# Prompt attention on one core: value products of a unit in one run, a unit later, with wider exponentials and score tiles in a borrowed ring

## The chip, the cores and the metric

One core of a Trainium2 chip runs the whole kernel in one launch. The metric is the device time of the kernel in microseconds (us). The times shown are the median of three timed runs, beside one execution that the hardware profiler recorded. PE is TensorE (matmuls), PEld its weight loads, DVE is VectorE, ACT ScalarE, POOL GpSimd and SP SyncE, which issues most DMAs.

## What is computed

One inference step of a decoder layer. 2048 prompt tokens and 8 x 8 new tokens go through one input projection, then through two groups of heads in parallel (eight forgetting-attention heads of width 64, four mLSTM heads of width 128), an output projection, LayerNorm and an MLP. The change concerns the prompt's attention:

```python
s = jnp.einsum('bqhd,bkhd->bhqk', q_i, k).astype(jnp.float32) * scale
s = s + L_i[..., :, None] - L[:, :, None, :]          # L: running sum of the log forget gate
s = jnp.where(k_pos[None, :] <= q_pos[:, None], s, -jnp.inf)
p = jax.nn.softmax(s, axis=-1)
return jnp.einsum('bhqk,bkhd->bqhd', p.astype(v.dtype), v)
```

The new tokens attend to 8192 cached positions each, whose pages are gathered from memory. That stream of gathers runs beside the other stages.

## The kernel before

The stages follow one another: input projection with the mLSTM scan beside it (phase A), prompt attention (phase B), output projection (phase O), MLP (phase C). The program is written with a tile scheduler: the order of the instructions on each engine is decided when the kernel is built, from the order in the source, the room in the pools and a model of time; on the chip each engine works through its own list and waits where a semaphore says so.

**Phase B** (`phase_b`) works in 64 units, one for a head h and a group g of 256 queries (two tiles of 128). In loop round n it computes `scores` of unit n and `values` of unit n - 1 (`LA = 1`).

- `scores(z, g)`: for each of the two query tiles, keys in blocks of 512. Two matmuls a block (L1074, L1075; the query is split into a high and a low part) go into a PSUM bank `pS`, of which three are in turn. DVE adds the forget term and takes the row's maximum on the way into an SBUF tile `S` (L1081; L1085 for the diagonal block). `S` tiles have 512 columns and ten buffers. POOL prepares the diagonal's mask `nd` (L1067).
- `values(z, g, sc)`: ACT takes the exponential of each `S` tile in place, up to 512 columns at a time, with the row's sum (L1100). Then, for each four key tiles: PE transposes four 128 x 128 weights into a PSUM bank `pt` (L1113, three banks), ACT or DVE copies them to an SBUF tile `PT` (L1116, L1118; four buffers), and PE multiplies them with the values `vn` (L1122). Key tile k adds to the lower 64 partitions of `po` if k is even, to the upper 64 if it is odd (`c = (k % 2) * 64`). A unit has nk = 2g + 2 key tiles, so 2 to 16 value products, 576 in all; the last one covers only the second query tile (128 columns). At the end the halves are added (L1128, L1130), and after four units `finish` divides by the sums and stores.
- Beside them stand the loads and splits of the next unit's queries (`queries`) and the transposes and splits of the next head's keys (`keys`, L1030).

Two things of other stages are issued from the loop. `kx["ring"]` (six slots of 1024 columns) belongs to the stream of cached keys; the first six gathers into it (L1637, on POOL) go out one in each of the rounds 10 to 15, and the stream goes on in phase O. Four loads of `w_o` (L1213, on SP) into the pool `raw()` (`wr`, four buffers of 1024 columns) are asked for in round 12; phase O starts with them, as with the loads of `xr` from `dmix` (L1268).

Of the kernel before, what the change touches and what calls it, by code (L numbers as in the profile page):

```python
# [10 lines left out]
F32 = mybir.dt.float32  # L11
# [14 lines left out]
S = 2048  # L26
# [26 lines left out]
def body(ctx, tc, I, O, stages):  # L53
    nc = tc.nc
    V, A, G, T, SY = nc.vector, nc.scalar, nc.gpsimd, nc.tensor, nc.sync
# [20 lines left out]
    ident = cst.tile([128, 128], F32, name="ident")  # L76
# [24 lines left out]
    acc = [0.0, None, PACE_A, None]  # L101
    macc = [0.0, [], PACE_M]
    last = {}

    vx = dict(more=None, live=[], next=0, of={})
    kx = dict(ring=None, new=False, free=False)
# [7 lines left out]
    def beside(gen):  # L114

        with ExitStack() as es:
            for i in last.values():
                es.enter_context(tc.issue_after(i.ins))
            return next(gen, 0)

    def attend():

        r = beside(acc[1])
        if r == 3:
            acc[3] = acc[1]
        if r in (0, 3):
            acc[1] = None

    def tick(us):

        macc[0] += us
        while macc[1] and macc[0] > macc[2]:
            macc[0] -= macc[2]
            if beside(macc[1][0]) == 0:
                macc[1].pop(0)
        if not macc[1]:
            macc[0] = 0.0
        acc[0] += us
        while acc[1] is not None and acc[0] > acc[2]:
            acc[0] -= acc[2]  # L140
            attend()
# [817 lines left out]
    for bi in range(4):  # L959
        g = block_a(bi)  # L960
# [18 lines left out]
    def phase_b():  # L979
        es = ExitStack()  # L980
        pb = es.enter_context(tc.tile_pool(name="pb", bufs=1, reuse_waits="tile"))
        ppb = es.enter_context(tc.tile_pool(name="ppb", bufs=1, space=PSUM, reuse_waits="tile"))
# [69 lines left out]

        lastnd = [None]

        def scores(z, g):

            qh, ql = z.pop(("q", g))
            ks = z["ks"]
            forget = lambda a, b: Bz["nl"][:, a:b] if z["h"] == 0 and a < 512 else z["nl"][:, a:b]
            out = []  # L1060
            for i in range(2):
                qt = 2 * g + i
                n = (qt + 1) * 128
                qs = slice(i * 128, i * 128 + 128)
                mx = pb.tile([128, 8], F32, name="mx", bufs=8)
                nd = pb.tile([128, 128], F32, name="nd", bufs=3)
                lastnd[0] = G.tensor_tensor(nd, forget(qt * 128, n), dmask, op=OP.add)  # L1067
                st = []
                j = 0
                for a in range(0, n, 512):  # L1070
                    b = min(n, a + 512)
                    w = max(b - a, 256)
                    pS = bank()
                    T.matmul(pS[:, :w], qh[:, qs], ks[:, a:a + w], start=True, stop=False)  # L1074
                    last["PE"] = T.matmul(pS[:, :w], ql[:, qs], ks[:, a:a + w], start=False, stop=True)  # L1075
                    tick(0.42)
                    sp = pb.tile([128, 512], F32, name="S", bufs=10)
                    st.append(sp)
                    e = min(b, qt * 128)
                    if e > a:  # L1080
                        last["DVE"] = V.tensor_tensor_reduce(out=sp[:, :e - a], in0=pS[:, :e - a], in1=forget(a, e), scale=1.0, scalar=NEG,  # L1081
                                               op0=OP.add, op1=OP.max, accum_out=mx[:, j:j + 1])
                        j += 1
                    if b == n:
                        V.tensor_tensor_reduce(out=sp[:, e - a:b - a], in0=pS[:, e - a:b - a], in1=nd, scale=1.0, scalar=NEG,  # L1085
                                               op0=OP.add, op1=OP.max, accum_out=mx[:, j:j + 1])
                        j += 1
                V.tensor_reduce(mx[:, 7:8], mx[:, :j], axis=AX.X, op=OP.max, negate=True)  # L1088
                out.append((st, mx))
            return out  # L1090

        def values(z, g, sc):

            for i, (st, mx) in enumerate(sc):
                qt = 2 * g + i
                n = (qt + 1) * 128
                lp = pb.tile([128, 4], F32, name="lp", bufs=8)
                for k, sp in enumerate(st):
                    w = min(512, n - k * 512)
                    last["ACT"] = A.activation(sp[:, :w], sp[:, :w], AF.Exp, bias=mx[:, 7:8], accum_out=lp[:, k:k + 1])  # L1100
                V.tensor_reduce(z["ls"][:, qt:qt + 1], lp[:, :len(st)], axis=AX.X, op=OP.add)

            po = ppb.tile([128, 256], F32, name="po", bufs=1)
            nk = 2 * g + 2
            for k0 in range(0, nk, 4):
                PT = pb.tile([128, 4, 256], F32, name="PT", bufs=4)
                for i in range(2):
                    kk = min(4, 2 * g + i + 1 - k0)
                    if kk <= 0:
                        continue  # L1110
                    pt = ppb.tile([128, 4, 128], F32, name="pt", bufs=3)
                    for k in range(kk):
                        T.transpose(pt[:, k], sc[i][0][k0 // 4][:, k * 128:(k + 1) * 128], ident)  # L1113
                    dst = PT[:, :kk, i * 128:i * 128 + 128]
                    if i == 0 or (k0 // 4) % 2 != 0:
                        A.copy(dst, pt[:, :kk])  # L1116
                    else:
                        V.tensor_copy(dst, pt[:, :kk])  # L1118
                for k in range(k0, min(k0 + 4, nk)):
                    q0 = 128 if k == nk - 1 else 0  # L1120
                    c = (k % 2) * 64
                    last["PE"] = T.matmul(po[c:c + 64, q0:], z["vn"][:, k], PT[:, k - k0, q0:],  # L1122
                                          start=(k < 2), stop=(k >= nk - 2), skip_group_check=True)
                tick(0.45 * min(4, nk - k0))
            if g % 4 == 0:
                z["ot"] = pb.tile([64, 1024], F32, name="ot", bufs=2)
            od = z["ot"][:, (g % 4) * 256:(g % 4) * 256 + 256]
            A.copy(od, po[0:64])  # L1128
            q0 = 128 if g == 0 else 0
            V.tensor_tensor(od[:, q0:], od[:, q0:], po[64:128, q0:], op=OP.add)  # L1130
            if g % 4 == 3:
                finish(z, g // 4)
# [19 lines left out]
        units = [(h, g) for h in range(8) for g in range(8)]  # L1152

        Z = {0: dict(h=0)}
# [4 lines left out]
        V.memset(dmask, 0.0)  # L1159
        G.affine_select(dmask, dmask, pattern=[[-1, 128]], compare_op=OP.is_ge, fill=NEG, base=0, channel_multiplier=1)  # L1160
        keys(Z[0], 0, kn)
        sc = {}
        LA = 1
        for n in range(len(units) + LA):
            if 10 <= n < 16 and acc[1] is not None:

                with tc.issue_after(lastnd[0].ins):
                    attend()
            if n == 12:
                wo.extend(half_wo(0, q) for q in range(4))  # L1170
            if n < len(units):
                h, g = units[n]
                sc[n] = scores(Z[h], g)
                if h == 0 and g % 2 == 0 and g < 6:
                    keys(Z[0], g // 2 + 1)
                if h < 7:
                    if g == 3:
                        Z[h + 1] = head(h + 1)
                        forget_values(Z[h + 1], 0, S)
                    if g >= 4:  # L1180
                        keys(Z[h + 1], g - 4)
                if n + 1 < len(units):
                    queries(Z[units[n + 1][0]], units[n + 1][1])
            if n >= LA:
                h, g = units[n - LA]
                values(Z[h], g, sc.pop(n - LA))
        es.close()
        es_z.close()

# [12 lines left out]
    def raw():  # L1202

        return pcw.tile([128, 1024], F32, name="wr", bufs=4)
# [295 lines left out]
def sample_attention(tc, I, O, ps_, pps, cst, ident, sqk, dnl, dR, dmix, dqb, vx, kx, pe, ring_a):  # L1500
# [226 lines left out]
    def weights(b, u, hg):  # L1727

        z = state[b]
        if hg == 0:  # L1730
            z["PT"] = ps_.tile([128, 2, 4, 4, 4, 8], F32, name="PTs", tag="PTs", bufs=1)
        PT = z["PT"]
        p = pps.tile([128, 4, 128], F32, name="sT", tag="sX", bufs=1)
        for f in range(4):
            T.transpose(p[:, f], z["U"][u][:, hg, f].rearrange("p k t -> p (k t)"), ident)
        for f in range(4):
            (A.copy if f % 2 else V.tensor_copy)(PT[:, hg, f].rearrange("p g h q -> p h g q"),
                                                 p[:, f].rearrange("p (h g q) -> p h g q", g=4, q=8))
# [22 lines left out]
    def pv_step(b, kt, after):  # L1761
# [9 lines left out]
        for n, f in enumerate((1, 0)):  # L1771
            with ExitStack() as es:
                if after is not None:
                    es.enter_context(tc.issue_after(after.ins))
                for g in range(2):
                    for hg in range(2):
                        r = (g * 2 + hg) * 32
                        after_ = T.matmul(po[r:r + 32], z["PT"][:, hg, 2 * f + g, pg].rearrange("p h q -> p (h q)"),  # L1778
                                          vts[f][:, g, hg * 256:(hg + 1) * 256], start=(kt == 0 and n == 0),
# [117 lines left out]
```

## Time and profile before

| what | us |
| --- | --- |
| median of three timed runs | 3359.53 (3354.93 to 3370.77) |
| the profiled execution, its own time | 3340.76 |
| its span, first to last instruction | 3339.1 |
| prompt attention in it, by the first and last of its matmuls | 922 to 1365 |

How to read it: a line of a group shows line, engine, operation, what it writes and reads, shape and count, then its busy time in us and the mean of one in ns, then the engine's idle time ahead of it and what ended that. Value products and other full-precision products leave two records for one product. Matmul ends are modelled, so distances between starts say more than durations. A row of the timeline merges instructions of one line that follow each other; it shows the first start, the time from there to the last end, and the count of records.

### The profile page before, as it was taken

To read this page: it belongs to the slowest core of one execution; us is meant where nothing else is said; L and a number is where in the kernel's file an instruction comes from. 1 tells how busy PE (TensorE), PEld (TensorE's weight loads), DVE (VectorE), ACT (ScalarE), POOL (GpSimd) and SP (SyncE) were. 2 spreads that over 40 slices of the span, in tenths; PEclk is the share of its full clock that TensorE was granted. 3 is DMA by queue.
4 is the path that set the end of the run, shared out by engine and by line. 5 is a ranking of instruction groups with operands and counts; after the bars stand their busy time and mean duration, and the time that the engine had idled before them with its cause. 6 is when DMAs were issued, how large, how long until landed. Compare 5 with 4: busy or idle time off the path is not lost. (4 is left out here: it accounts for less than half of the span.)

```text
span 3339.1 us, 57487 instructions
## 1 busy us (share of the span) xinstructions
PE 3231.6 (97%) x21420; PEld 2604.3 (78%) x21420; DVE 2156.3 (65%) x5225; ACT 1413.0 (42%) x2990; POOL 869.9 (26%) x932
## 2 busy tenths in 40 slices
PE   9999999999989999999999998999999999999998
PEld 8998797887866666677777776777777777889997
DVE  6857667566477878655666667666676545755555
ACT  4444245344278888422333333232433333433332
POOL 0112122422332322376432324323243210100001
PEclk9999999999999999999999999999999999999999
DMA  5666765967652322587776768767678654442221
GB/s 174 166 189 187 219 207 186 300 218 233 213 167 81 91 76 58 200 293 255 278 265 240 247 216 301 271 238 254 233 244 312 200 172 142 154 140 82 89 83 67
DMA packets 427296, 646.24 MB, mean 194 GB/s; under 512 B 83148, under 2 KB 320016, under 8 KB 426120
## 3 DMA queue, kind: packets, MB, share of 16 engines
q1 hardware_dynamic: 350184, 363.09, 36.0%
q0 software_dynamic: 74304, 270.57, 22.0%
q10 hardware_dynamic: 2528, 8.91, 0.7%
q8 instruction: 169, 2.77, 0.3%
q14 instruction: 111, 0.91, 0.1%
HBM read 589.63 MB, written 52.83 MB: 192 GB/s over the span
## 5 line engine op out<-in xcount | busy, mean ns | idle before, releaser
L1458 DVE TENSOR_TENSOR y<-y,py 128x512 f32<-128x512 f32 x475 | 320.0, 680 | 275.6 <-PE py L159 260.5
L149 ACT ACTIVATE wh<-wr 128x1024 fp32r<-128x1024 f32 x268 | 279.5, 1057 | 511.5 <-PE py L159 262.2
L1643 DVE STREAM_TRANSPOSE kT<-kT 128x512 f32<-128x512 f32 x512 | 330.6, 685 | 206.2 <-DMA kT<-cache_k,idxK 205.3
L157 PE MATMUL ph<-x1h,wh 128*128 128x512 f32 (+1 forms) x1280 | 454.2, 355 | 3.0 <-ACT wh L149 2.3
L1637 POOL DMA_INDIRECT kT<-cache_k,idxK x256 | 270.7, 1057 | 715.5 <-PE sQ L1666 651.7
L159 PE MATMUL ph<-x1h,wl 128*128 128x512 f32 (+1 forms) x1280 | 451.6, 354 | 4.9 <-DVE wl L152 4.8
L158 PE MATMUL ph<-x1l,wh 128*128 128x512 f32 (+1 forms) x1280 | 453.8, 355 | 0.0
L157 PE MATMUL py<-wh,h 128*128 128x512 f32 x1024 | 406.5, 399 | 5.9 <-DVE y L1456 4.5
L158 PE MATMUL py<-wl,h 128*128 128x512 f32 x1024 | 400.9, 392 | 0.0
L159 PE MATMUL py<-wh,h 128*128 128x512 f32 x1024 | 400.9, 392 | 0.0
L152 DVE TENSOR_TENSOR wl<-wr,wh 128x1024 fp32r<-128x1024 f32 x268 | 336.0, 1259 | 88.4 <-PE ph L159 34.4
L157 PE MATMUL pm<-whi,xhT 128*128 128x256 f32 (+2 forms) x1040 | 303.1, 291 | 1.6 <-DVE xlT L152 1.0
L159 PE MATMUL pm<-whi,xlT 128*128 128x256 f32 (+2 forms) x1040 | 298.3, 287 | 0.0
L158 PE MATMUL pm<-wlo,xhT 128*128 128x256 f32 (+2 forms) x1040 | 298.1, 287 | 0.0
L157 PEld LDWEIGHTS ph<-x1h,wh 128*128 128x128 f32 x1280 | 241.6, 189 | 40.6 <-issue 4.1
L159 PEld LDWEIGHTS ph<-x1h,wl 128*128 128x128 f32 x1280 | 241.2, 188 | 40.1 <-DVE wl L152 6.6
L158 PEld LDWEIGHTS ph<-x1l,wh 128*128 128x128 f32 x1280 | 241.4, 189 | 35.5 <-issue 4.1
L157 PEld LDWEIGHTS py<-wh,h 128*128 128x128 f32 x1024 | 192.3, 188 | 61.1 <-issue 11.5
L159 PEld LDWEIGHTS py<-wh,h 128*128 128x128 f32 x1024 | 192.2, 188 | 45.1 <-issue 4.1
L158 PEld LDWEIGHTS py<-wl,h 128*128 128x128 f32 x1024 | 192.4, 188 | 35.8 <-DVE wl L152 0.4
L1100 ACT ACTIVATE S<-S,mx 128x512 f32<-128x512 f32 (+2 forms) x320 | 207.9, 653 | 18.5 <-DVE mx L1088 17.9
L1754 POOL DMA_INDIRECT vt<-cache_v,idxV x158 | 163.1, 1032 | 194.5 <-PE sO L1778 138.2
(410 smaller groups left out, 6668.5 us busy)
## 6 DMA issues: line engine op xcount, KB each, us to landing
wr<-w SPq DMA_DIRECT2D x256, 512.0 KB
wra<-w_in SPq DMA_DIRECT2D x112, 512.0 KB
Rb<-dR SPq DMA_DIRECT2D x128, 128.0 KB
wr<-w_o SPq DMA_DIRECT2D x16, 512.0 KB
xr<-dmix SPq DMA_DIRECT2D x16, 512.0 KB
y<-x_prompt SPq DMA_DIRECT2D x16, 512.0 KB
dx<-y SPq DMA_DIRECT2D x16, 512.0 KB
xr<-dx SPq DMA_DIRECT2D x16, 512.0 KB
```

The costliest lines, as they stand in the source:

```text
L149: last["ACT"] = A.activation(dst, src, AF.Copy, scale=scale)
L152: r = (eng or V).tensor_tensor(dst, src, hi.bitcast(F32), op=OP.subtract)
L157: T.matmul(ps, wh, xh, start=first, stop=False)
L158: T.matmul(ps, wh, xl, start=False, stop=False)
L159: last["PE"] = T.matmul(ps, wl, xh, start=False, stop=stop)
L1100: last["ACT"] = A.activation(sp[:, :w], sp[:, :w], AF.Exp, bias=mx[:, 7:8], accum_out=lp[:, k:k + 1])
L1458: V.tensor_tensor(y, y, ps, op=OP.add)
L1637: G.indirect_dma_start(out=piece(n), out_offset=None, in_=ck, in_offset=IO(ap=idxK[:, b, j // 2, j % 2:j % 2 + 1], axis=0))
L1643: V.transpose(x, x)
L1754: G.indirect_dma_start(out=vt.rearrange("p f c -> p (f c)"), out_offset=None, in_=cv, in_offset=IO(ap=idxV[:, b, (kt % 4) * 4 + kt // 4, f ...
```

## The change

Scores are placed by `place`: tiles of 1024 columns, alternately in five buffers of `S` and in the six slots of the key ring, up to round 54; from round 55 on only in `S`. `values` is cut in two. `weights` takes exponentials of up to 1024 columns and makes all transposes of a unit, into `PT` tiles for every other unit and into lent `wr` buffers for the others (while n is at most 60). The new `values` multiplies in one go, in the order nk-2, 0, 1, ..., nk-3, nk-1, one round later, and is put behind the last score matmul of the round before on PE's list. The last units (n over 60) multiply at once. The six gathers move to rounds 56 to 61, the four `w_o` loads to round 62.

```diff
+        GATHER = 56
+        taken = [0]
+        def place(n):
+            i = taken[0] % 12
+            taken[0] += 1
+            if i % 2 == 0 or n >= GATHER - 1:
+                return pb.tile([128, 1024], F32, name="S", bufs=5)
+            return kx["ring"][:, i // 4, i // 2 % 2]
...
-                    sp = pb.tile([128, 512], F32, name="S", bufs=10)
-                    st.append(sp)
+                    if a % 1024 == 0:
+                        st.append(place(n_))
+                    sp = st[-1][:, a % 1024:a % 1024 + 512]
...
-        def values(z, g, sc):
+        def weights(z, g, sc, lent):
...
-                    w = min(512, n - k * 512)
+                    w = min(1024, n - k * 1024)
...
-                PT = pb.tile([128, 4, 256], F32, name="PT", bufs=4)
+                PT = raw().rearrange("p (k c) -> p k c", k=4) if lent else pb.tile([128, 4, 256], F32, name="PT", bufs=4)
+                PTs.append(PT)
...
-                        T.transpose(pt[:, k], sc[i][0][k0 // 4][:, k * 128:(k + 1) * 128], ident)
+                        T.transpose(pt[:, k], sc[i][0][k0 // 8][:, (k0 % 8 + k) * 128:(k0 % 8 + k + 1) * 128], ident)
...
-                for k in range(k0, min(k0 + 4, nk)):
-                    q0 = 128 if k == nk - 1 else 0
-                    c = (k % 2) * 64
-                    last["PE"] = T.matmul(po[c:c + 64, q0:], z["vn"][:, k], PT[:, k - k0, q0:],
-                                          start=(k < 2), stop=(k >= nk - 2), skip_group_check=True)
-                tick(0.45 * min(4, nk - k0))
+            return PTs
+
+        def values(z, g, PTs):
+            po = ppb.tile([128, 256], F32, name="po", bufs=1)
+            nk = 2 * g + 2
+            ks = [nk - 2, *range(nk - 2), nk - 1]
+            for n, k in enumerate(ks):
+                q0 = 128 if k == nk - 1 else 0
+                c = (k % 2) * 64
+                same = [i for i in ks if i % 2 == k % 2]
+                last["PE"] = T.matmul(po[c:c + 64, q0:], z["vn"][:, k], PTs[k // 4][:, k % 4, q0:],
+                                      start=k == same[0], stop=k == same[-1], skip_group_check=True)
...
-        for n in range(len(units) + LA):
-            if 10 <= n < 16 and acc[1] is not None:
+        for n in range(len(units) + 1):
+            if GATHER <= n < GATHER + 6 and acc[1] is not None:
                 with tc.issue_after(lastnd[0].ins):
                     attend()
-            if n == 12:
+            if n - 2 in PTs:
+                with tc.issue_after(final[0].ins):
+                    values_of(n - 2)
+            if n == END + 2:
                 wo.extend(half_wo(0, q) for q in range(4))
...
-            if n >= LA:
-                h, g = units[n - LA]
-                values(Z[h], g, sc.pop(n - LA))
+            if n > 0:
+                h, g = units[n - 1]
+                PTs[n - 1] = weights(Z[h], g, sc.pop(n - 1), n % 2 == 0 and n <= END)
+                if n > END:
+                    values_of(n - 1)
```

More of the change, by code (lines that the diff above doesn't have):

```diff
@@ L1053, in phase_b, with scores @@
         lastnd = [None]
-        def scores(z, g):
+        GATHER = 56
[6 more added lines that the diff above has]
+            return kx["ring"][:, i // 4, i // 2 % 2]
+        def scores(z, g, n_):
             qh, ql = z.pop(("q", g))
@@ L1098, in values @@
                 for k, sp in enumerate(st):
-                    w = min(512, n - k * 512)
+                    w = min(1024, n - k * 1024)
                     last["ACT"] = A.activation(sp[:, :w], sp[:, :w], AF.Exp, bias=mx[:, 7:8], accum_out=lp[:, k:k + 1])
                 V.tensor_reduce(z["ls"][:, qt:qt + 1], lp[:, :len(st)], axis=AX.X, op=OP.add)
-            po = ppb.tile([128, 256], F32, name="po", bufs=1)
             nk = 2 * g + 2
+            PTs = []
             for k0 in range(0, nk, 4):
-                PT = pb.tile([128, 4, 256], F32, name="PT", bufs=4)
+                PT = raw().rearrange("p (k c) -> p k c", k=4) if lent else pb.tile([128, 4, 256], F32, name="PT", bufs=4)
+                PTs.append(PT)
                 for i in range(2):
@@ L1161, in phase_b, with values_of @@
         keys(Z[0], 0, kn)
-        sc = {}
-        LA = 1
-        for n in range(len(units) + LA):
-            if 10 <= n < 16 and acc[1] is not None:
+        sc, PTs, final = {}, {}, [None]
+        END = 60
+        def values_of(n):
+            h, g = units[n]
+            values(Z[h], g, PTs.pop(n))
+        for n in range(len(units) + 1):
+            if GATHER <= n < GATHER + 6 and acc[1] is not None:
                 with tc.issue_after(lastnd[0].ins):
                     attend()
-            if n == 12:
+            if n - 2 in PTs:
+                with tc.issue_after(final[0].ins):
+                    values_of(n - 2)
+            if n == END + 2:
                 wo.extend(half_wo(0, q) for q in range(4))
@@ L1172, in phase_b @@
                 h, g = units[n]
-                sc[n] = scores(Z[h], g)
+                sc[n] = scores(Z[h], g, n)
+                final[0] = last["PE"]
                 if h == 0 and g % 2 == 0 and g < 6:
```

## The prediction

> **What bounds the kernel now.** The page's first lines come first. Its chain of waits is no help here: it names only the last 2 us of the kernel. So I asked for the busy time of the stretches around prompt attention, the only stage that the diff rewrites.
>
> ```profile
> PE 3231.6 (97%) x21420; PEld 2604.3 (78%) x21420; DVE 2156.3 (65%) x5225; ACT 1413.0 (42%) x2990; POOL 869.9 (26%) x932
> ```
>
> ```profile
> 922.00:950.00 28.00, 21.08 (x114) 14.67 (x114) 19.54 (x80) 16.65 (x50) 6.10 (x15) 0.88 0.88 249
> 950.00:1357.00 407.00, 406.50 (x2837) 281.91 (x2836) 323.04 (x1288) 343.45 (x961) 113.32 (x184) 1.00 0.29 80
> 1357.00:1367.00 10.00, 7.24 (x57) 4.51 (x55) 3.77 (x9) 6.50 (x14) 2.52 (x2) 1.00 0.12 36
> 922.00:1367.00 445.00, 434.82 (x3004) 301.09 (x3004) 346.35 (x1376) 366.61 (x1023) 121.95 (x201) 0.99 0.32 90
> ```
>
> In the second view the columns are the stretch, its length, busy us of PE, PEld, DVE, ACT, POOL, the granted clock, DMA share and GB/s. The stage is the 445 us from 922 to 1367, 13% of the span. From 950 to 1357 PE is busy for 406.5 of 407 us at full clock; DVE has 323 us of work, ACT 343, and DMA 29%. PE waits only at the two ends, 6.9 us and 2.8 us. But a busy PE can still lose time inside its own stream, so I asked for the groups of the stage by form, and then for PE alone in order of time.
>
> ```profile
> L1113 PE MATMUL pt<-ident,S 128*128 128x128 f32 x1088 | 172.3, 279 | 2.5 <-DVE mx L1088 1.1 <-DVE PT L1118 0.4 <-DVE ks L152 0.2
> L1122 PE MATMUL po<-PT,vn 128*64 128x256 f32 x1024 | 153.9, 392 | 0.1
> L1122 PE MATMUL po<-PT,vn 128*64 128x128 f32 x128 | 25.9, 284 | 0.0
> ```
>
> ```profile
> 1203.00 0.49 PE L1113 MATMUL pt<-ident,S 128*128 128x128 f32 x3
> 1203.42 1.95 PE L1122 MATMUL po<-PT,vn 128*64 128x256 f32 x16
> 1205.30 0.66 PE L1113 MATMUL pt<-ident,S 128*128 128x128 f32 x4
> 1205.89 1.08 PE L1122 MATMUL po<-PT,vn 128*64 128x256 f32 x8
> 1206.90 0.33 PE L1113 MATMUL pt<-ident,S 128*128 128x128 f32 x1
> ...
> 1285.10 0.60 PE L1113 MATMUL pt<-ident,S 128*128 128x128 f32 x4
> 1285.46 0.48 PE L1074 MATMUL pS<-ks,qh 128*128 128x512 f32 x1
> ...
> 1288.10 1.03 PE L1113 MATMUL pt<-ident,S 128*128 128x128 f32 x8
> 1288.89 0.36 PE L1074 MATMUL pS<-ks,qh 128*128 128x256 f32 x1
> ```
>
> A value product writes 64 columns of the array (128*64), the lower and the upper half in turn, and leaves two records (1152 for 576 products). The distance between starts tells what a run of them costs. Eight products (x16) hold PE from 1203.42 to 1205.30, 1.88 us; four (x8) from 1205.89 to 1206.90, 1.01 us. So one more product costs 0.217 us, and a run has 1.01 - 4*0.217 = 0.14 us of its own. The neighbours pay as well: the four transposes between the two runs hold PE from 1205.30 to 1205.89, 0.59 us. Among their like, eight take 0.79 us up to the score behind them (1288.10 to 1288.89) and four 0.36 us (1285.10 to 1285.46), so four more cost 0.43 us. That is another 0.16 us for leaving one run and entering the next. **Each run of value products costs 0.30 us beyond its work**, hidden in busy time.
>
> **The change, part by part.** *One run per unit.* The instruction listings of both programs give PE's order, which is fixed when the kernel is built. Before, the 576 products stand in 134 runs (85 of four, 24 of two, 17 of eight, 7 of six, one of ten). After, they stand in 69: one for each of 64 units, five of them split by a few transposes. PE has the same 1212 transposes and 640 score matmuls. 65 runs go: 65 * 0.30 = **-19.5 us**.
>
> *Order inside a run.* It was 0, 1, 2, ...; it is now nk-2 first, then 0 to nk-3, and nk-1 last. So two products of the lower half stand at the head and two of the upper half at the end. Now two halves work side by side: 0.217 us a product is far below the 0.39 us of a single one of its two records. If each half keeps a queue of its own, both still have nk/2 products, and the order costs 0. If products must start in listed order, the first works alone (2*0.217 = 0.43 us), the last, half as wide, alone too (0.22 us), and one pair is saved (0.43 us): +0.21 us in each of the 56 units with over two products, +12 us. A run with a wide and a narrow product shows which; the view was cut at 1199.69, 1199.70 and 1199.90:
>
> ```profile
> 1199.53 0.43 PE L1122 MATMUL po<-PT,vn 128*64 128x256 f32 x2
> 1199.53 0.44 PE L1122 MATMUL po<-PT,vn 128*64 128x256 f32 x3
> 1199.53 0.65 PE L1122 MATMUL po<-PT,vn 128*64 128x256 f32 x4
> ```
>
> The third record starts at 1199.69 to 1199.70 and all three have ended by 1199.97, so it took 0.28 us: by the rows of forms above that is a narrow one (284 ns; a wide one has 392). The fourth ends at 1200.18. The narrow product, second in the listing, began its second half before the wide one did. So the halves do not wait for each other, at least over one product. I take 0 and keep 12 for the range. The Trainium skill ("TensorE: Matmul & The Clock Gate", Part 3) says that matmuls start and end strictly in program order. By that rule the +12 us would be paid; the three rows speak against it.
>
> *Exponentials of up to 1024 columns.* 320 become 192.
>
> ```profile
> L1100 ACT ACTIVATE S<-S,mx 128x512 f32<-128x512 f32 x224 | 160.3, 718 | 16.1 <-DVE mx L1088 15.6
> L1100 ACT ACTIVATE S<-S,mx 128x256 f32<-128x256 f32 x32 | 15.9, 498 | 0.1
> L1100 ACT ACTIVATION_READ_ACCUMULATOR S<-S,mx 128x1 f32 x320 | 61.2, 191 | 0.0
> L1081 DVE CUSTOM_DVE_ANT_0 S<-pS,nl 128x512 f32<-128x512 f32 x192 | 129.9, 684 | 24.2 <-PE pt L1113 15.4 <-PE pS L1075 7.7
> L1118 DVE COPY PT<-pt 128x512 f32<-128x512 f32 x80 | 55.1, 689 | 10.0 <-PE pt L1113 8.4
> L1116 ACT COPY PT<-pt 128x512 f32<-128x512 f32 x144 | 82.2, 581 | 23.3 <-PE pt L1113 21.7
> ```
>
> 256 columns more cost 220 ns, so an exponential has 278 ns of fixed cost, and its accumulator read 191 ns: 128 * 0.47 = 60 us less on ACT. PE hides all of it (ACT waits 21.7 us for transposes): 0. By the first two rows a 1024-column exponential would take about 1.16 us (an estimate), 0.44 us more than now, and a copy of transposes queued behind it on ACT waits that much longer. Three transpose banks hold 12 transposes, 1.3 us of PE, so that is covered except in a burst. If PE waited the 0.44 us in each of 64 units: +28 us. The row nearest to it is ACT's waiting for PE and not PE for ACT, so I take it near nothing (below).
>
> *Waits that longer runs bring.* While PE runs up to 16 products (0.14 + 16*0.217 = 3.6 us) it makes no scores and no transposes, and DVE and ACT live on what stands in the three score and three transpose banks: 3 * 0.68 us of scores and some copies. DVE is loaded to 346 of 445 us now (78%), and to 81% with 19.5 us gone. Bounds: 0, as in 950 to 1357 where PE waits 0.5 us; and 55 us (rival 2). I take the nearer row: 3 us over the stage, **+3 us**.
>
> *Score tiles in the key ring, wr lent for transposed weights.* 5 tiles of 1024 columns take the room of 10 of 512, and six ring slots come on top: more room for scores ahead, up to unit 55. From then on the units share five tiles, freed 1024 columns at a time; that is in the 3 us. If PE waits a 512-column evacuation (0.68 us) in each of the last eight units instead, it costs 5 us.
>
> *Moved transfers.* The six gathers into the ring go from unit 10 to unit 56, the four w_o loads from unit 12 to unit 62 of the loop (by the clock they went out as early as 940).
>
> ```profile
> 980.71 1.27 POOL L1637 DMA_INDIRECT kT<-cache_k,idxK  x1 [0.17 <-issue]
> 1009.13 1.01 POOL L1637 DMA_INDIRECT kT<-cache_k,idxK  x1 [0.16 <-issue]
> DMA to landing us min/median/max: 4.5/4.6/4.7
> 940.49 2.12 SPq L1213 DMA_DIRECT2D wr<-w_o  x4
> 1331.86 1.02 SPq L1268 DMA_DIRECT2D xr<-dmix  x2
> ```
>
> A gather holds POOL for 1.0 us and lands 4.6 us later (first and last of six shown). Behind it on POOL stands only the next diagonal sum, made a unit ahead. In the new listing the w_o loads stand on SP just before the transfers that end in the xr<-dmix loads; no query load is left behind them. They wait for value products of units 55 to 59, so they go out at about the time of that row, 1332, some 30 us before w_o is used (1366): 2 MB at the 249 GB/s of the first stretch is 8.4 us. Cost 0; if they came after PE's end instead, +8 us. At the front, where DMA is 88% busy, the 2 MB leave; that is part of rival 4, and I take 0.
>
> **Sum:** -19.5 + 0 + 3 = -16.5 us. The profiled execution took 3340.8 us (span 3339.1), so 3324.3. The three timed runs have a median of 3359.5 (3354.9 to 3370.8), 18.7 us above it, so **3343 us** on that footing, 0.49% faster. 0.5%, 16.8 us, is about what a measurement of this kernel can tell from no change, and the forecast sits on it.
>
> **Rivals.** *1. The ends of a run work alone* (order within a run): -19.5 + 12 + 3 = -4.5 us, 3355. For: two products of one half do stand together. Against: the narrow record that overtook.
>
> *2. DVE starves in the long runs, and PE pays between them* (slower). DVE has 346.35/8 = 43.3 us of work a head, and a head would last (445 - 19.5)/8 = 53.2 us, so it may idle 9.9 us. The eight runs of a head last 0.58 to 3.62 us, 16.8 us together. If one score bank (0.68 us) is full when a run begins, DVE idles 11.4 us, 1.5 too many: +12 us a stage, still faster. If none is, 16.8 us: 6.9 too many a head, +55 us, and the kernel at 3359.5 - 19.5 + 55 = 3395 us. It gets slower than before once under about 0.55 us of work is in the banks. For: the new order has six to twelve transposes right before some runs, during which DVE empties the score banks. Against: others have two or three scores right before.
>
> *3. DVE or ACT becomes the bound and the 19.5 us turn into waits*: 3359. Against: with 19.5 us gone DVE is loaded to 81%, and ACT, without its 60 us, to 72%.
>
> *4. PE's waits at the two ends go too*, 6.9 and 2.8 us, since ACT has less to do: -29 us, 3330. Against: at the front most of it is for the first loads, which stay.
>
> *5. ACT is the bound.* Then its 60 us would count: 3300. PE's 0.5 us of waiting in 407 speaks against it. The Trainium skill ("Perfetto Trace Analysis", Identifying the Most-Contended Engine) calls busy matmul time a bad measure and judges PE by the share of its weight loads. By that rule ACT (366.6 of 445) would stand before PE (301.1).
>
> **How the numbers follow.** Forecast 0.55, half of it beyond 0.5%; rival 1 0.13; 2 0.12; 3 0.09; 4 0.08; 5 0.03. Faster: 0.275 + 0.08 + 0.03, about 0.39; slower 0.12; within 0.5% 0.49. The range leaves out rivals 2 and 5, 0.15 together. It reaches from rival 4 less the spread of the timed runs below their median (3330 - 5) to rival 3 with their spread above it (3359.5 + 11); the +28 us bound of the longer exponentials also ends there (-19.5 + 28 + 3 = +11.5).
>
> **What would show it.** Right: about 69 runs of value products, x32 for the longest; the stage some 16 us shorter with PE still waiting for nearly nothing in its middle; exponentials of 1024 columns near 1.16 us. Order inside a run: starts in pairs from the first product on; for rival 1 the first and the last alone. For rival 2, PE waits that name score evacuations, right behind long runs. Wrong altogether: any change of time outside 922 to 1367, such as w_o landing late at the next stage's start.

## The result, and the profile after

The changed kernel takes 3355.1 us (median of 20 runs, 3343.5 to 3368.4), the kernel before 3363.6 us (20 runs, 3354.9 to 3371.0) on the same chip: ratio 0.9972, 95% interval 0.9962 to 0.9983. A second set gave 0.9964 (0.9950 to 0.9978). So it is some 0.3% faster, 9 to 12 us, where 16.5 us was forecast. The profiled execution of after took 3345.25 us (span 3343.5) against 3340.76 before: the stage that the diff rewrites got shorter in it, the stages around it longer, by amounts that also differ between profiles of one kernel. From here on the stage is measured by itself, from the start of its first score matmul to the start of its last value product: 922.43 to 1364.40 before, 442.0 us (440.8 in a second profile), and 929.85 to 1359.56 after, 429.7 us (429.0). That is 12.0 us less by the means of the two, inside the interval of both timed comparisons (5.7 to 12.8 and 7.4 to 16.7 us).

The first line of after's page, then its busy time by stretches (columns as in the prediction):

```profile
PE 3227.1 (97%) x21420; PEld 2633.3 (79%) x21420; DVE 2153.3 (64%) x5225; ACT 1379.5 (41%) x2734; POOL 871.0 (26%) x932
```

```profile
929.00:957.00 28.00, 21.88 (x124) 15.54 (x124) 21.05 (x91) 16.55 (x43) 7.92 (x19) 0.94 0.69 185
957.00:1350.00 393.00, 389.75 (x2807) 304.36 (x2808) 319.89 (x1279) 311.36 (x714) 111.35 (x181) 1.00 0.31 88
1350.00:1363.00 13.00, 9.60 (x78) 6.90 (x75) 4.59 (x9) 7.59 (x13) 3.21 (x3) 0.99 0.12 31
929.00:1363.00 434.00, 421.23 (x3005) 326.80 (x3005) 345.53 (x1376) 335.50 (x769) 122.47 (x203) 1.00 0.33 92
```

In the middle PE now stands idle for 3.25 of 393 us; before it was 0.5 of 407. That is only the idle time between modelled matmuls. The groups of the stage by form show the new exponentials and both places of the transposed weights (`PT` and the lent `wr`):

```profile
L1126 PE MATMUL pt<-ident,S 128*128 128x128 f32 x711 | 105.0, 277 | 1.0 <-DVE PT L1131 0.5 <-ACT PT L1129 0.3 <-DVE wr L1131 0.2
L1112 ACT ACTIVATE S<-S,mx 128x1024 f32<-128x1024 f32 x67 | 77.1, 1150 | 21.4 <-DVE mx L1100 19.6 <-DVE ls L1113 1.7
L1143 PE MATMUL po<-wr,vn 128*64 128x256 f32 x524 | 69.7, 387 | 0.4 <-DVE ot L1150 0.4
L1143 PE MATMUL po<-PT,vn 128*64 128x256 f32 x500 | 69.4, 388 | 1.5 <-ACT PT L1129 1.5
```

An exponential of 1024 columns takes 1.15 us (1.16 was estimated). PE's timeline shows value products in long runs:

```profile
996.07 3.67 PE L1143 MATMUL po<-wr,vn 128*64 128x256 f32 x32
999.66 0.55 PE L1126 MATMUL pt<-ident,S 128*128 128x128 f32 x3
...
1006.26 1.08 PE L1143 MATMUL po<-wr,vn 128*64 128x256 f32 x8
1007.27 0.50 PE L1085 MATMUL pS<-ks,qh 128*128 128x512 f32 x1
...
1016.00 1.94 PE L1143 MATMUL po<-wr,vn 128*64 128x256 f32 x16
1017.88 0.33 PE L1126 MATMUL pt<-ident,kT 128*128 128x128 f32 x1
```

Four products hold PE for 1.01 us, eight for 1.88, sixteen for 3.59: the prediction's 0.14 + 0.217 a product gives 1.01, 1.88 and 3.61. The 576 products stand in 69 runs, as listed.

PE's idle time understates waiting. For a better measure I took, for each matmul in the stage, the distance from its start to the next start. From it I took the usual short distance, which is the 20th percentile, in before and after together, of all places where the same three kinds of matmul follow each other (the one ahead, this one and the next, told apart by what they write and by shape). What is left over 25 ns was summed, outside the runs. These **waits** are 10.2 us in the first 28 us, 2.0 in the middle and 1.2 in the last 15 before; 8.2, 8.8 and 2.4 after. The stage without them is the **rest**. Two profiles each:

| | stage | waits | rest |
| --- | --- | --- | --- |
| before | 442.0, 440.8 | 13.4, 12.5 | 428.6, 428.3 |
| after | 429.7, 429.0 | 19.4, 18.6 | 410.3, 410.4 |

So the runs gave 18.1 us, and 6.1 us of it came back as waits.

Where they come back is seen at a place that returns once a head: the run of the unit g = 5 (x24), behind which the scores of the next head's shortest units follow. First after's timeline of PE, then those of DVE and ACT:

```profile
1081.28 2.80 PE L1143 MATMUL po<-wr,vn 128*64 128x256 f32 x24
1084.01 1.09 PE L1126 MATMUL pt<-ident,S 128*128 128x128 f32 x8
...
1088.26 0.28 PE L1086 MATMUL pS<-ks,ql 128*128 128x256 f32 x1
1089.06 0.47 PE L1085 MATMUL pS<-ks,qh 128*128 128x512 f32 x1 [0.52 <-DVE mx L1100]
```

```profile
1083.57 0.43 DVE L152 TENSOR_TENSOR ql<-qn,qh 128x256 fp32r<-128x256 f32 x1 [0.59 <-ACT qh L149]
1084.70 0.69 DVE L1131 COPY PT<-pt 128x512 f32<-128x512 f32 x1 [0.70 <-PE pt L1126]
...
1088.62 0.28 DVE L1097 CUSTOM_DVE_ANT_0 kT<-pS,nd 128x128 f32<-128x128 f32 x1
1088.83 0.15 DVE L1100 TENSOR_REDUCE mx<-mx 128x1 f32<-128x2 f32 x1
```

```profile
1083.44 1.14 ACT L1112 ACTIVATE S<-S,mx 128x1024 f32<-128x1024 f32 x1
...
1084.57 1.14 ACT L1112 ACTIVATE kT<-kT,mx 128x1024 f32<-128x1024 f32 x1
...
1085.96 0.59 ACT L1129 COPY PT<-pt 128x512 f32<-128x512 f32 x1
```

PE makes no score in the 2.7 us of products. DVE stands idle for 0.59 us near their end, until ACT has split the next queries (`qh`), and for 0.70 us more behind them, until the first four transposes are there. Behind the run twelve score matmuls and 21 transposes come within 5 us, for short rows that need many small instructions. DVE is still at its row maxima when PE wants a bank, and PE waits 0.52 us. ACT has two long exponentials ahead of it, and the next copy of transposes starts only at 1085.96, 2 us after PE went on. Of the fourteen largest waits of the middle (0.24 to 0.68 us each) six stand at such places, at 1035.9, 1088.3, 1140.1, 1141.2, 1192.6 and 1244.2; four stand at 964 to 985 and four in the last head (1301 to 1328). By the same measure 4.6 of the 8.8 us of middle waits lie between a run of g = 5 and the run behind it, and 4.6 of 8.6 in the second profile. Behind the longest runs (x32) there are none in the middle. So the length of a run alone doesn't make the wait; what stands behind it counts as well.

### The profile page after: what moved, and what is told of

Its sections match the earlier page's. It is cut to its first block, busy times and chain, and to the rows that moved or that the text cites. A ratio compares the mean times of both kernels' runs of the same rounds, so it can differ in the third digit from the quotient of the medians.

```text
span 3343.5 us, 57217 instructions
## 1 busy us (share of the span) xinstructions
PE 3227.1 (97%) x21420; PEld 2633.3 (79%) x21420; DVE 2153.3 (64%) x5225; ACT 1379.5 (41%) x2734; POOL 871.0 (26%) x932
## 3 DMA queue, kind: packets, MB, share of 16 engines
q8 instruction: 169, 2.77, 0.3%
## 5 line engine op out<-in xcount | busy, mean ns | idle before, releaser
L157 PEld LDWEIGHTS py<-wh,h 128*128 128x128 f32 x1024 | 192.2, 188 | 58.3 <-issue 13.1
L157 PEld LDWEIGHTS pm<-whi,xhT 128*128 128x128 f32 (+1 forms) x1040 | 198.9, 191 | 10.6 <-issue 6.6
```

The lines of the kernel that those rows point to most:

```text
L157: T.matmul(ps, wh, xh, start=first, stop=False)
```

## The experiments

The theory after the result: a run costs what was predicted, and PE waits behind some of the longer runs because DVE and ACT together can't catch up there. The rivals: the order inside a run costs something (rival 1 of the prediction), DVE alone is short (rival 2), the waits are latency whatever the load, or time was lost outside the stage.

| kernel | runs of products | stage, us | waits first / middle / last | ratio to before (95%) |
| --- | --- | --- | --- | --- |
| before | 134 | 442.0 | 10.2 / 2.0 / 1.2 | 1 |
| before_again | 134 | 440.8 | 9.3 / 2.0 / 1.2 | one run |
| after | 69 | 429.7 | 8.2 / 8.8 / 2.4 | 0.9972 (0.9962 to 0.9983) |
| after_again | 69 | 429.0 | 7.6 / 8.6 / 2.4 | 0.9964 (0.9950 to 0.9978) |
| natural_order | 122 | 440.1 | 8.7 / 4.2 / 1.0 | 1.0013 (1.0000 to 1.0026) |
| exp_512 | 66 | 435.5 | 8.8 / 13.8 / 3.0 | 0.9992 (0.9981 to 1.0004) |
| no_ring | 64 | 438.3 | 8.5 / 19.0 / 2.4 | 0.9992 (0.9982 to 1.0002) |
| onerun_only | 64 | 449.0 | 8.8 / 27.7 / 2.5 | 1.0025 (1.0012 to 1.0038) |
| wide_only | 150 | 454.0 | 9.3 / 5.7 / 1.0 | 1.0052 (1.0034 to 1.0069) |
| copies_to_act | 65 | 429.4 | 8.1 / 9.9 / 2.7 | 0.9961 (0.9945 to 0.9977) |
| copies_small | 65 | 429.1 | 7.4 / 10.7 / 2.1 | 0.9962 (0.9948 to 0.9976) |
| light_exp | 65 | 419.6 | 7.0 / 2.5 / 1.5 | one run |
| merged_small | 55 | 426.0 | 7.6 / 7.1 / 2.1 | 0.9961 (0.9946 to 0.9976) |
| merge2 | 56 | 428.7 | 8.7 / 9.9 / 2.4 | 0.9965 (0.9952 to 0.9977) |

Each ratio is to the runs of before in the same set.

**after_again and before_again: the two kernels once more.**

> The changed kernel once more, to see how far two profiles of one program agree. The stage (first score matmul to last value product) took 442.0 us before and 429.7 us after: 19.5 us less by 65 fewer runs of value products, some 7 us more of PE's waits. Again 429.7 within 1.5 us, if that is the program's own; a stage of 425 or 435 would make the 7 us a matter of one execution. Ratio to before 0.997.

> The kernel before, unchanged, profiled once more. Every theory rests on its stage of 442.0 us (first score to last value product), so both expect 441 to 443 and waits of about 10 / 2 / 1 us (first 28 us, middle, last 15 us). If it lies over 2 us away, the shares of the stage given so far have to be given with that spread.

The stages repeat within 0.7 and 1.2 us, the middle waits within 0.2 us. What follows is read from differences of over 2 us.

**natural_order: the products of a run in the order 0, 1, 2, ...**

```diff
-            ks = [nk - 2, *range(nk - 2), nk - 1]
+            ks = [*range(nk)]
```

> As the changed kernel, but the products of a unit in the order 0, 1, 2, ... again. By the listing the scheduler then breaks the runs: 122 instead of 69. If a run costs 0.30 us, PE gets 53 * 0.30 = 15.9 us more, and loses most of the 7 us of new waits, since runs are short again: stage 439 to 446 us, ratio to before 0.999 to 1.001. If instead the order at the ends of a run costs (products of one half working alone, 12 us), this kernel is faster than the changed one: stage near 418 us.

The gain is gone, though no single run got longer or shorter: eight products take 1.87 us in both orders. In natural order the first products need only the first transposes, and the tile scheduler sends them ahead: 122 runs instead of 69. The rest of the stage is 440.1 - 13.9 = 426.2 us, 15.9 us above after's 410.3, for 53 runs: 0.30 us each, the predicted price. The order nk-2 first asks for the last group of transposes at the head of the run, and so keeps the run whole. The single starts in both traces show why it costs nothing by itself: the records of a run start in pairs from the first product on, 0, 14, 267, 280, 483, 496 ns in after, although its first two products are both of the lower half, and 0, 7, 267, 273, 482, 489 ns in natural order.

**exp_512: after with exponentials of up to 512 columns.**

```diff
-                    last["ACT"] = A.activation(sp[:, :w], sp[:, :w], AF.Exp, bias=mx[:, 7:8], accum_out=lp[:, k:k + 1])
+                    for c in range(0, w, 512):
+                        e = min(c + 512, w)
+                        last["ACT"] = A.activation(sp[:, c:e], sp[:, c:e], AF.Exp, bias=mx[:, 7:8],
+                                                   accum_out=lp[:, 2 * k + c // 512:2 * k + c // 512 + 1])
-                V.tensor_reduce(z["ls"][:, qt:qt + 1], lp[:, :len(st)], axis=AX.X, op=OP.add)
+                V.tensor_reduce(z["ls"][:, qt:qt + 1], lp[:, :(n + 511) // 512], axis=AX.X, op=OP.add)
```

> As the changed kernel, but exponentials of 512 columns again (320 instead of 192), 66 runs. ACT has 60 us more to do. If PE binds and the new waits come from DVE, the stage stays at 427 to 431 us. If the long exponentials hold up ACT's copies of the transposes and so make the waits, they shrink: 424 us. If ACT is near its limit, the stage grows by 10 us or more.

Half of the gain is gone. The middle of its stage:

```profile
957.00:1350.00 393.00, 387.06 (x2780) 300.20 (x2777) 319.36 (x1264) 336.64 (x943) 109.19 (x181) 1.00 0.31 88
```

ACT works 25 us more than after's 311.36 and is still busy for only 86% of the time; yet the middle waits rise from 8.8 to 13.8 us. So in the new order the wide exponentials are worth about 6 us of the stage.

**no_ring: after with all score tiles in the five buffers of S.**

```diff
-            if i % 2 == 0 or n >= GATHER - 1:
+            if True:
```

> As the changed kernel, but score tiles only in the five S buffers, never in the ring; 64 runs. If the room of the ring is needed to carry DVE and ACT over the long runs, PE's waits grow beyond the 8.8 us in the middle of the stage: stage 433 to 440 us. If not, it is 428 us, by the five runs fewer.

```profile
957.00:1350.00 393.00, 386.11 (x2756) 296.41 (x2754) 312.69 (x1253) 305.73 (x700) 113.42 (x182) 1.00 0.31 88
```

PE idles 6.9 us in this stretch, in after 3.25; the middle waits rise to 19.0 us, the stage to 438.3: the borrowed room is worth 9 us.

**onerun_only: before with the products behind all transposes of their unit, nk-2 first, and nothing else.**

```diff
+            PTs = []
             for k0 in range(0, nk, 4):
                 PT = pb.tile([128, 4, 256], F32, name="PT", bufs=4)
+                PTs.append(PT)
...
-                for k in range(k0, min(k0 + 4, nk)):
...
-                    last["PE"] = T.matmul(po[c:c + 64, q0:], z["vn"][:, k], PT[:, k - k0, q0:],
-                                          start=(k < 2), stop=(k >= nk - 2), skip_group_check=True)
-                tick(0.45 * min(4, nk - k0))
+            ks = [nk - 2, *range(nk - 2), nk - 1]
+            for k in ks:
...
+                last["PE"] = T.matmul(po[c:c + 64, q0:], z["vn"][:, k], PTs[k // 4][:, k % 4, q0:],
+                                      start=k == same[0], stop=k == same[-1], skip_group_check=True)
```

> As the kernel before, with one part of the change alone: all transposes of a unit first, then its products in one run, in the same loop round, with exponentials and score tiles of 512 columns and no ring. 64 runs: 70 * 0.30 = 21 us off PE. But the run now waits for the copy of its last transposes (0.6 to 0.7 us) and PE has only ten score tiles to work ahead in. If being a unit late and the room are what makes the runs pay, PE waits most of it back: stage 433 to 445 us. If the runs alone do it: near 422 us and no more waits than before.

```profile
957.00:1350.00 393.00, 383.58 (x2676) 287.72 (x2674) 315.28 (x1239) 323.41 (x921) 110.88 (x182) 1.00 0.29 83
```

64 runs and a rest of 410.0 us as in after, but PE idles 9.4 us in this stretch, and the middle waits are 27.7 us: the stage takes 449.0 us, more than the 445 expected. Alone, the one run per unit makes the kernel slower. The three other parts (a unit late, wide exponentials, room) take 19 us of these waits away.

**wide_only: before with exponentials of up to 1024 columns in five tiles of 1024, and nothing else.**

```diff
-                    sp = pb.tile([128, 512], F32, name="S", bufs=10)
-                    st.append(sp)
+                    if a % 1024 == 0:
+                        st.append(pb.tile([128, 1024], F32, name="S", bufs=5))
+                    sp = st[-1][:, a % 1024:a % 1024 + 512]
...
-                    w = min(512, n - k * 512)
+                    w = min(1024, n - k * 1024)
...
-                        T.transpose(pt[:, k], sc[i][0][k0 // 4][:, k * 128:(k + 1) * 128], ident)
+                        T.transpose(pt[:, k], sc[i][0][k0 // 8][:, (k0 % 8 + k) * 128:(k0 % 8 + k + 1) * 128], ident)
```

> Of the change only the exponentials of up to 1024 columns, with score tiles of 1024 columns (five of them); value products stay in runs of up to four as before. The listing has 16 runs of value products more than before, by the price of 0.30 us +4.8 us. Theory (the wide exponentials help only where PE's long runs leave ACT too little time, and the room is no larger here): PE's middle waits stay near the 2 us of before, the stage takes 442.0 + 4.8 = 447 us, the kernel 1.001 to 1.002 of before. Rival (the 6 us that the kernel with exponentials of 512 columns lost is what wide ones are worth in any order): 447 - 6 = 441 us, and a ratio just under 1.

Slower by 0.52%, more than either expected: 12.6 us above the mean of before's two profiles. 16 more runs make 4.8 us, 3.1 us are new waits (the middle has 4.2 us of them between two transposes), and 4.7 us remain in the rest. These go with an order in which scores and transposes take turns less often (a score follows a transpose at 135 places, at 235 before; a matmul starts about 0.06 us behind the transpose ahead of it there, against 0.12 us between two transposes). That last link is only read from the sums, not tried by itself, and after speaks against it: there a score follows a transpose at 159 places, 76 fewer than before, and the rest still fell by 0.28 us a run. So the cause of the 4.7 us stays open. Wide exponentials help only beside the long runs.

**copies_to_act and copies_small: copies of transposes taken from DVE to ACT, all past the first four of a unit, or those of the units g = 7, 0, 1 and 2.**

```diff
-                    if i == 0 or (k0 // 4) % 2 != 0:
+                    if i == 0 or k0 != 0:                                       # copies_to_act
+                    if i == 0 or (k0 // 4) % 2 != 0 or g in (7, 0, 1, 2):       # copies_small
```

> As the changed kernel, but the copies of the third group of transposes go to ACT as well: 24 * 0.69 + 8 * 0.42 = 20 us off DVE, 17 us onto ACT, 65 runs. If the new waits of PE (8.8 us in the middle of the stage, 2.0 before) come from DVE falling behind after long runs, half of them go: stage near 424 us, ratio 0.995. If they come from ACT, they grow: 432 us or more.

> As the changed kernel, but the copies of transposes of units g = 7, 0, 1 and 2 all go to ACT: 25 us off DVE just where PE's new waits stand (the small units after a head's longest run, where DVE comes out of the run with many short operations to do); 65 runs. If DVE's arrears after long runs make the waits, the stage (429.0 and 429.7 us in two profiles of the changed kernel) goes to 424 to 427 us. If it is ACT's queue, as the 6 us lost with short exponentials may say, it goes to 432 us or more.

In the stretch from 957 to 1350 DVE's busy time falls from 319.9 us to 306.9 and 305.9, less than the 20 and 25 us expected, and ACT's rises from 311.4 to 320.5 and 323.7. Neither changes the stage by more than 0.6 us. The middle waits even rise by 1 to 2 us; four runs fewer make up for it. If DVE alone were what PE waits for, the waits would have fallen.

**light_exp: after with exponentials of only 128 columns, and DVE's copies past the first four on ACT.**

```diff
+                    w = 128
                     last["ACT"] = A.activation(sp[:, :w], sp[:, :w], AF.Exp, bias=mx[:, 7:8], accum_out=lp[:, k:k + 1])
...
-                    if i == 0 or (k0 // 4) % 2 != 0:
+                    if i == 0 or k0 != 0:
...
-            V.reciprocal(lr, ls)
+            V.tensor_scalar(lr, ls, 0.0, None, op0=OP.mult)
```

> The changed kernel with ACT and DVE both made lighter: each exponential covers only the first 128 columns of its tile (the rest stay as scores), all copies of transposes past the first four go to ACT, and the reciprocal of the sums is a multiplication by zero. ACT has some 100 us less of exponentials in the stage, DVE some 25 us less of copies. Theory (the 7 us of new waits in the middle are PE waiting for DVE and ACT together, who have too little time and room beside long runs): middle waits fall from 8.8 to 2 to 3 us and the stage from 429.7 to about 423 us, with run counts nearly those of the changed kernel (four runs fewer, -1.2). Rival (the waits are latency: a short unit behind a long run needs its score, its exponential, its transpose and its copy one after another, whatever the engines' load): they shrink only by what a shorter exponential takes off that chain and stay at 6 us or more, the stage at 427 or more.

This kernel leaves out most of the exponentials and the division by the sums, so what it computes is no longer the attention; it serves to make ACT light. The middle of its stage by busy time:

```profile
958.00:1340.00 382.00, 381.05 (x2790) 303.06 (x2789) 302.24 (x1250) 237.83 (x742) 111.65 (x181) 1.00 0.31 89
```

ACT has 238 of 382 us to do, and PE idles 0.95 us again. Middle waits fall to 2.5 us and the stage to 419.6, with a rest of 408.6. Against copies_to_act, which has the same copies and the same number of runs, the exponentials differ, and besides them only the reciprocals (16 in the stage, 0.35 us each there and 0.18 here on DVE): 9.9 us of middle waits against 2.5. The rest is the same in both (408.6 and 408.7). So the new waits hang mainly on the time that ACT needs for exponentials, and the latency theory (6 us or more would stay) is out in that form. Whether ACT's load counts or the length of one exponential (0.40 us by the row below, whose line 1113 is the exponential, and 1.15 in after) this run alone doesn't tell; exp_512, with shorter exponentials and more load, waits more, which speaks for the load. How much of the waits a lighter DVE would take away stays open.

```profile
L1113 ACT ACTIVATE S<-S,mx 128x128 f32<-128x128 f32 x110 | 44.2, 402 | 35.4 <-DVE mx L1100 34.7
```

**merged_small and merge2: the products of units 0 and 1, and of 2 and 3, of each of the first seven heads in one run; merged_small moves copies as copies_small does.**

```diff
-            po = ppb.tile([128, 256], F32, name="po", bufs=1)
...
+            po = ppb.tile([128, 512], F32, name="po", bufs=1)
+            o = 0 if before is None else 256
+            todo = []
+            for u, P, a in ((g - 1, before, 0), (g, PTs, o)):
+                if P is not None:
...
+                    todo += [(u, P, a, ks, k) for k in ks]
...
+            for u, P, a, ks, k in todo:
...
-            values(Z[h], g, PTs.pop(n))
+            values(Z[h], g, PTs.pop(n), PTs.pop(n - 1, None))
...
-            if n - 2 in PTs:
+            if n - 2 in PTs and not (n - 2 < END - 4 and units[n - 2][1] in TOP):     # TOP = (0, 2)
```

> A version that may beat both: as copies_small, and the products of units g = 0 and 1, and of 2 and 3, stand in one run each (one PSUM tile for both, one copy out): 55 runs, 14 fewer than the changed kernel, -4.2 us, and fewer copies out. By the price of a run alone: stage 425 us; with DVE's arrears gone too, 420 to 423 us. If longer runs starve DVE more than they save, 430 us or more.

> The changed kernel with the value products of the two shortest pairs of units of a head (units 0 and 1, 2 and 3) in one run, copies divided between ACT and DVE as in the changed kernel. 13 runs fewer in the listing than the changed kernel: 13 * 0.30 = 3.9 us. Theory (price of a run, with waits unchanged): the stage takes 429.4 - 3.9 = 425.5 us and the kernel 0.996 of before. Rival (each merge makes a longer run behind which DVE and ACT run dry, so that the gain turns into waits): middle waits rise by 4 us, the stage stays at 429.

Ten runs fewer than copies_small shorten the stage by 3.1 us, but its rest stays (409.2 against 408.9): what goes is waits. Thirteen fewer than after shorten merge2's by 0.7, no more than two profiles of one kernel differ, with 2.6 us less rest (0.20 us a run) and 2 us more waits. Below 69 runs the price doesn't come out in full any more, why isn't settled, and neither kernel can be told from after by its time (0.9961 and 0.9965).

## Why the prediction was right and wrong

*The price of a run was right.* -19.5 us was forecast for 65 runs, and the rest of the stage fell by 18.1 us, 0.28 us a run; natural_order gives 0.30 over 53.

*The order inside a run at 0 was right, and rival 1 is out.* The records of a run start in pairs from the first one on, and no run got longer (eight products 1.87 us in both orders). By the strict program order of the Trainium skill ("TensorE: Matmul & The Clock Gate", Part 3) the first product would run alone; these starts and the unchanged length of the runs speak against it here. What the prediction missed is what the order is worth to the scheduler: without it the run falls apart, and 10.7 us with it.

*The step that failed is "I take the nearer row: 3 us over the stage".* The waits that longer runs bring measured 6.1 us (middle +6.7, last 15 us +1.2, first 28 us -1.9, by the mean of two profiles). The row that I leaned on, 0.5 us of idle time in 407, came from an order in which a run never held PE for over 2.3 us, and it counts only idle time, while 2.0 us of waits stood there even then. The neighbour on the other side, rival 2, had half of the mechanism: DVE stands idle at a long run and is late behind it. But more than half of the middle waits lie at one place a head, none behind the longest runs, and the engine that light_exp shows short is ACT, which rival 2 didn't count. With -18.1 + 6.1 the stage moves by -12.0 us in place of -16.5: 3.1 us of the miss are waits, 1.4 us the price of a run.

*Two prices of zero were right in the sum and wrong as prices.* The wide exponentials were to bring nothing and the borrowed room nothing past 5 us: taken out of the changed kernel they cost 6 and 9 us. Both keep the term of the waits small, which without one of them would be 13 or 17 us. The 60 us less on ACT were 33.5 (1413.0 to 1379.5 over the kernel). The timeline of ACT in after shows why:

```profile
1080.50 1.14 ACT L1112 ACTIVATE S<-S,mx 128x1024 f32<-128x1024 f32 x1
1081.54 0.19 ACT L1112 ACTIVATION_READ_ACCUMULATOR S<-S,mx 128x1 f32 x1
1081.63 1.03 ACT L1112 ACTIVATE kT<-kT,mx 128x896 f32<-128x896 f32 x1
```

The read of the sum begins 0.10 us before the exponential has ended, and the next exponential 0.10 us before the read has. Of 0.47 us for an exponential and its read, 0.2 us lie beside others.

*The moved transfers at 0 were right.* From the last value product to PE's next matmul of phase O it is 2.76 us before and 2.77 us after. The w_o loads went out at 1321.8 to 1324.2, before the loads of `xr` at 1332.6.

*Time outside the stage, the sign of being wrong altogether, is not settled to the last few us.* The stage begins at 922.4 and 924.7 us in before's two profiles and at 929.9 in both of after's, but at 933.0 in onerun_only, whose source ahead of the stage is before's. From the last value product to the end it is 1974.7 and 1975.1 us before, 1984.0 and 1975.4 after. The timed gain (5.7 to 12.8 and 7.4 to 16.7 us) has room for the whole 12.0, so no loss outside is shown, and none of a few us is excluded. The interval also tells more than the prediction allowed it: it reaches some 0.1% to either side, where 0.5% was taken as what a measurement can tell from no change.

*The other rivals.* 3 (all turned into waits): a third of the gain did, not all. 4 (waits at the ends go too): the first 28 us lost 1.9 us of waits, the end gained 1.2. 5 (ACT is the bound): taking most of the exponentials away from copies_to_act brings 9.8 us, nearly all of it waits: 7.4 us in the middle, where its long runs had made 7.9 new ones. Before, PE waited 2 us there. ACT bounds some places of the new order, not the stage.

## What to carry to other kernels

A run of matmuls that write only part of the array has a price of its own, here 0.28 to 0.30 us, which can be read from the distances between starts in a trace in which PE looks busy all the time; fewer and longer runs save it. But a long run starves the engines that feed on PE's other work, so price it with what those engines have in hand when it begins and with the work that stands right behind it, and take the number of an idle engine in the old order as a floor only. Parts that look worthless one by one (a wider instruction, borrowed buffers) can be what keeps the gain, and a reordering is worth what the scheduler makes of it, so count the runs in the listing that was built.

## What was not expected of the hardware

Two products of the same half of the array at the head of a run start no later than two of different halves: the second pair of records at 267 and 280 ns with the order nk-2, 0, 1, and at 267 and 273 ns with the order 0, 1, 2. The halves also keep up over a whole run: sixteen products with one more of the lower half first and one of the upper half last take 3.60 us, as 0.14 + 16 x 0.217 gives. A score matmul starts about 0.06 us behind the transpose ahead of it (235 steps in 13.1 us before), where a transpose behind a transpose takes 0.12 us (910 in 109.1).
